# Feed-forward products of a decoder step by one level of Strassen's algorithm, up units first

## The chip, the cores and the metric

The kernel runs on one core of a Trainium2 chip. The time is that of the whole launch on the device in microseconds (us), as a median over runs; lower is better. Engines are named as the profile names them: PE is TensorE, with PEld for its weight loads, DVE is VectorE, ACT is ScalarE, POOL is GpSimd, and SP is SyncE, which here only issues transfers.

## The reference

One step of a gated decoder layer for 1024 prompt tokens and 8 x 8 sample tokens, all in float32, 1088 token columns in all:

```
u = rmsnorm(x);  [a | q | k | v | g_a | g_b] = u @ w_in            # w_in: 1024 x 4864
A = causal multi-scale pooling of a  @ w_pa
B = dilated sliding-window attention of q, k, v and the caches  @ w_pb
h = x + (sigmoid(g_a) * A + sigmoid(g_b) * B) @ w_o                # 1024 x 1024
y = h + relu(rmsnorm(h) @ w_up)^2 @ w_down                         # 1024 x 4096, 4096 x 1024
```

Outputs are y and the updated pooling states and key-value caches. The last two lines are what the change touches.

## The kernel before

All of it works on transposed activations: 128 channels on the partitions, tokens along the free axis. The 1088 tokens are cut into CHUNKS of 384, 384 and 320 columns. Every matmul operand is held as two fp32r parts, a high and a low one, and every product is made in three passes (high by high, high by low, low by high; `PASSES`, L132, `gemm`, L141 to L150, the matmul in L148). `split` (L104 to L107) makes the parts: ACT copies the value into the high part (L105), DVE subtracts that from the value for the low part (L106).

Weights come in panels of 128 x 2048 (`panel`, L114 to L127): four transfers of 256 KB on SP's queue, each split into one of three rotating `places`. `throttle` collects the last split of each panel; the copies of the caches to the outputs (L1202 to L1212, 44 transfers of some 1 MB on POOL's queue) wait for one such split each, from the fourteenth on, so that they go out one to a panel.

The stage of w_o (L1132 to L1152) makes `y` = h in SBUF, one tile of 128 x 1088 for each of eight channel blocks, chunk by chunk, and sums its squares into `sqa`. In its last panel and in the first feed-forward unit the closures in `todo` are called between the matmuls, one chunk at a time: `norm_sums` (column sums of `sqa` by PE, mean on DVE, power -1/2 on POOL), `split_h` (h times ln2, split into `act[0]` and `act[1]`), and `norm_spread` (a diagonal matrix on DVE, spread over the partitions by PE, copied to `rbh` by ACT).

The feed-forward loop (L1156 to L1199) has 16 units f, each for 256 of the 4096 hidden channels. An up half: the panel of w_up, six `gemm`s `pz` (three chunks by two blocks, 24 matmuls each), then r = max(pz, 0) * rbh on DVE (L1180), the square's high part on ACT (L1181), and its low part by two DVE operations (L1182, L1183) into `z`. A down half follows at once: the panel of w_down, 24 `gemm`s `py` of six matmuls each, and each sum is added to `y` in place by DVE (L1199). The last unit adds into rows in token order and stores them as `yT` (L1192 to L1196). Each half is 144 matmuls.

PE's instructions stand in the order of the code. On the other engines, the order is set when the program is built, by a scheduler that models times; each engine then takes its queue strictly in order, and transfers of one queue are issued in order, each waiting for what its buffers need.

Of the kernel before, what the change touches and what calls it, by code (L numbers as in the profile page):

```python
# [7 lines left out]
F32 = mybir.dt.float32  # L8
F32R = mybir.dt.float32r
# [23 lines left out]
def decoder_step(ctx, tc, i, o):  # L33
# [17 lines left out]
    cst = cp.tile([P, i["consts"].shape[1]], F32, name="cst")  # L51
    cols = cp.tile([P, i["cols"].shape[1]], F32, name="cols")
    off = [0]

    def take(n):
        r = cst[:, off[0]:off[0] + n]
        off[0] += n
        return r

    ident, m1, m3, halves, hmask, icnt, ms0, ms1, hsel, bsel = (take(n) for n in (128, 256, 128, 64, 1, 15, 136, 136, 4, 4))  # L60
# [39 lines left out]
    places = wp.tile([P, 3, 2, 2048], F32R, name="places")  # L100
    place = [0]
# [60 lines left out]
    acc_p = pool("acc", space=PSUM)  # L162
# [30 lines left out]
    xp = pa.enter_context(tc.tile_pool(name="pooling", bufs=1, side="right", reuse_waits="tile"))  # L193
    ap0 = pb.enter_context(tc.tile_pool(name="att0", bufs=1, reuse_waits="tile"))
# [165 lines left out]
    dma(cst, i["consts"])  # L360
# [731 lines left out]
    yp = pool("y", reuse_waits="tile")  # L1092
    y = [yp.tile([P, TOK], F32, name=f"y{k}") for k in range(KD)]
    rbh = yp.tile([P, TOK], F32, name="rbh")
    pd = ExitStack()
    hp = pd.enter_context(tc.tile_pool(name="h", bufs=1, side="right", reuse_waits="tile"))
    ps = pd.enter_context(tc.tile_pool(name="ps_d", bufs=1, space=PSUM, reuse_waits="tile"))
    sqa = [hp.tile([P, n], F32, name=f"sqa{c}") for c, (c0, n) in enumerate(CHUNKS)]
    hms = hp.tile([P, 9], F32, name="hms")
    hr = hp.tile([P, 9], F32, name="hr")  # L1100
    v_.memset(hr, 0.0)

    def norm_sums(c):
        n = CHUNKS[c][1]
        rt = ps.tile([P, 3], F32, name=f"rth{c}", tag="rt")
        for b in range(3):
            w = min(P, n - b * P)
            t_.matmul(rt[:w, b:b + 1], sqa[c][:, b * P:b * P + w], ones[:, :1], start=True, stop=True)
        for b, w in ((slice(0, n // P), P), (slice(n // P, 3), n % P)):
            if w and b.stop > b.start:  # L1110
                col = slice(3 * c + b.start, 3 * c + b.stop)
                v_.tensor_scalar(hms[:w, col], rt[:w, b], 1.0 / D, EPS, op0=ALU.mult, op1=ALU.add)
                g_.tensor_tensor(hr[:w, col], hms[:w, col], mhalf[:w, b], op=ALU.pow)

    def norm_spread(c):

        c0, n = CHUNKS[c]
        dg = rr(hp, [P, 3, P], F32, name=f"dg{c}", tag="dg", bufs=1)
        bc = ps.tile([P, 512], F32, name=f"bc{c}", tag="bc")
        spread(dg, hr, c, bc)  # L1120
        s_.copy(rbh[:, c0:c0 + n], bc[:, :n])

    def split_h(c):
        c0, n = CHUNKS[c]
        for k in range(KD):
            hi, lo = (act[s][k][:, c0:c0 + n] for s in range(2))
            behind_pe(s_.activation(hi, y[k][:, c0:c0 + n], AF.Copy, scale=ln2[:, k:k + 1]))
            v_.scalar_tensor_tensor(lo, y[k][:, c0:c0 + n], ln2[:, k:k + 1], hi.bitcast(F32),
                                    op0=ALU.mult, op1=ALU.subtract)

    todo = []
    for d in range(4):  # L1132
        wt = by_k(panel(i["w_o"][d], f"o{d}"))
        xr = rr(hp, [P, 2, TOK], F32, name=f"xr{d}", tag="xr", bufs=2)
        dma(xr, i["xT"][:, 2 * d:2 * d + 2])
        for c, (c0, n) in enumerate(CHUNKS):
            for m in range(2):
                kk = 2 * d + m
                po = acc_tile(f"ph{kk}_{c}")
                gemm(po[:, :n], KD, lambda s, k: wt[:, s, k, m * P:(m + 1) * P], lambda s, k: act[s][k][:, c0:c0 + n])  # L1140
                for here, row, toks in pieces(c):
                    v_.tensor_tensor(y[kk][:, row], po[:, here], xr[:, m, toks], op=ALU.add)
# [13 lines left out]
    NG = 16  # L1156
    fp = None
    for f in range(NG):
        wt = by_k(panel(i["w_up"][f], f"u{f}"))
        zz = []  # L1160
        for c, (c0, n) in enumerate(CHUNKS):
            pzs = []
            for m in range(2):
                pz = acc_tile(f"pz{f}_{c}_{m}")
                gemm(pz[:, :n], KD, lambda s, k: wt[:, s, k, m * P:(m + 1) * P], lambda s, k: act[s][k][:, c0:c0 + n])
                pzs.append(pz)
                if todo:
                    todo.pop(0)()
            if fp is None:
                while todo:  # L1170
                    todo.pop(0)()
                pd.close()
                fp = ctx.enter_context(tc.tile_pool(name="ffn", bufs=1, side="right", reuse_waits="tile"))
                ps = ctx.enter_context(tc.tile_pool(name="ps_e", bufs=1, space=PSUM, reuse_waits="tile"))
            z = rr(fp, [P, 2, 2, CH], F32R, name=f"z{f}_{c}", tag="z", bufs=4)
            zz.append(z)
            for m in range(2):
                r = rr(fp, [P, CH], F32, name=f"r{f}_{c}_{m}", tag="r", bufs=2)
                q = rr(fp, [P, CH], F32, name=f"q{f}_{c}_{m}", tag="q", bufs=2)
                v_.scalar_tensor_tensor(r[:, :n], pzs[m][:, :n], 0.0, rbh[:, c0:c0 + n], op0=ALU.max, op1=ALU.mult)  # L1180
                s_.activation(z[:, m, 0, :n], r[:, :n], AF.Square)  # L1181
                v_.tensor_tensor(q[:, :n], r[:, :n], r[:, :n], op=ALU.mult)  # L1182
                v_.tensor_tensor(z[:, m, 1, :n], q[:, :n], z[:, m, 0, :n].bitcast(F32), op=ALU.subtract)  # L1183
        wt = by_k(panel(i["w_down"][f], f"d{f}"), 2)
        final = f == NG - 1
        for c, k in [(c, k) for k in range(KD) for c in range(3)] if final else [(c, k) for c in range(3) for k in range(KD)]:
# [3 lines left out]
            if final:  # L1190

                row = y[k - 1] if k else rbh  # L1192
                for here, cols_, toks in pieces(c):
                    v_.tensor_tensor(row[:, toks], y[k][:, cols_], py[:, here], op=ALU.add)
                if c == 2:
                    dma_st(o["yT"][k * P:(k + 1) * P], row)  # L1196
# [115 lines left out]
```

## Time and profile before

| what | value |
|---|---|
| median of 3 runs | 1545.11 us (1544.89 to 1545.24) |
| span of the profiled execution, first to last instruction | 1543.0 us |
| time outside that span, against the median | 2.1 us |
| feed-forward stage, 32 halves of one unit | 757.9 us of the span |
| bytes moved by DMA | 178.66 MB, 116 GB/s on average |

The page gives busy times by engine over the span, the chain of work that ended last, groups of instructions with their mean durations, and the idle time ahead of them with what ended it. Busy times are averages over stages of very different kinds: attention keeps DVE, ACT and POOL busy, the feed-forward stage hardly uses POOL. What the change is worth is read from the feed-forward stage and its two ends.

### The profile page before, as it was taken

How to read it: one execution, taken by the hardware profiler on the slowest of the kernel's cores; microseconds unless marked ns; L12 is line 12 of the kernel's file. 1: busy time of each engine (PE TensorE's matmuls, PEld its weight loads, DVE VectorE, ACT ScalarE, POOL GpSimd, SP SyncE). 2: the span in 40 equal slices, each digit the busy share in tenths (PEclk: the TensorE clock that was granted, in tenths of full speed). 3: DMA queues.
4: the chain of work that ended last, by engine and by line, in shares of the span. 5: the costliest groups of instructions: out<-in, count | busy, mean ns of one | idle time of the engine just before them, and what ended most of it. 6: DMA issues, size and time to landing. Idle time of an engine off the chain costs nothing.

```text
span 1543.0 us, 25508 instructions
## 1 busy us (share of the span) xinstructions
PE 1519.3 (98%) x9779; PEld 1475.6 (96%) x9779; DVE 875.1 (57%) x1948; ACT 516.2 (33%) x1613; POOL 199.4 (13%) x245
## 2 busy tenths in 40 slices
PE   8999799899999999999999999999999999999998
PEld 8989788778999999999999999999999999999998
DVE  7555555858755444344575565555655556555556
ACT  8466655667763222222241111211111211112100
POOL 2611256545200000010010000000000000000000
PEclk9999899999999999999999999999999999999999
DMA  6212667765445443574331322313213223222102
GB/s 216 87 48 75 175 159 180 214 173 124 124 125 174 157 147 120 182 230 156 109 100 60 107 80 79 106 54 106 99 60 106 75 89 109 68 95 99 35 8 117
DMA packets 104536, 178.66 MB, mean 116 GB/s; under 512 B 16919, under 2 KB 69725, under 8 KB 103198
## 3 DMA queue, kind: packets, MB, share of 16 engines
q1 hardware_dynamic: 97870, 125.91, 27.0%
q0 software_dynamic: 6112, 50.33, 9.8%
q8 instruction: 77, 1.26, 0.3%
q10 hardware_dynamic: 432, 0.79, 0.1%
q14 instruction: 45, 0.37, 0.1%
HBM read 155.54 MB, written 65.10 MB: 143 GB/s over the span
## 4 chain that ended last, share of the span: by engine, by line
PE 92%; DMA 3%; DVE 2%; ACT 1%; issue 1%; POOL 1%; SPq 0%; DVEq 0%; POOLq 0%; ACTq 0%
PE py L148 25%; PE pz L148 24%; PE pga L148 6%; PE pgb L148 6%; PE ph L148 6%; PE pqk L148 5%; PE pv L148 3%; PE a L260 3%; PE pa L148 3%; DMA raw_qkv<-in_w_in_dram 2%; PE pb L148 2%; PE pk L148 1%; PE pq L148 1%; PE pog0b L623 1%; DMA pck<-in_cache_kv_dram 1%
## 5 line engine op out<-in xcount | busy, mean ns | idle before, releaser
L148 PE MATMUL pz<-act,places 128*128 128x384 f32 (+1 forms) x2304 | 382.4, 326 | 0.0
L148 PE MATMUL py<-z,places 128*128 128x384 f32 (+1 forms) x2304 | 381.6, 327 | 0.0
L148 PEld LDWEIGHTS pz<-act,places 128*128 128x128 f32 x2304 | 379.5, 188 | 0.4
L148 PEld LDWEIGHTS py<-z,places 128*128 128x128 f32 x2304 | 379.7, 188 | 0.0
L1199 DVE TENSOR_TENSOR y<-y,py 128x384 f32<-128x384 f32 (+1 forms) x360 | 187.9, 530 | 111.5 <-PE py L148 111.2
L1181 ACT ACTIVATE z<-r 128x384 fp32r<-128x384 f32 (+1 forms) x96 | 48.7, 508 | 321.9 <-DVE r L1180 321.9
L1180 DVE SCALAR_TENSOR_TENSOR r<-pz,rbh 128x384 f32<-128x384 f32 (+1 forms) x96 | 51.2, 534 | 168.8 <-PE pz L148 168.8
L1210 POOL DMA_DIRECT2D out_kv_sample_dram<-in_cache_kv_dram x44 | 21.8, 494 | 932.4 <-ACT places L105 910.8
L105 ACT ACTIVATE places<-raw_u 128x512 fp32r<-128x512 f32 x64 | 38.4, 627 | 266.9 <-PE py L148 258.6
L148 PE MATMUL pga<-act,places 128*128 128x384 f32 (+1 forms) x576 | 97.9, 328 | 0.0
L148 PE MATMUL pgb<-act,places 128*128 128x384 f32 (+1 forms) x576 | 97.8, 326 | 0.0
L148 PE MATMUL ph<-act,places 128*128 128x384 f32 (+1 forms) x576 | 95.9, 327 | 0.0
L148 PEld LDWEIGHTS pgb<-act,places 128*128 128x128 f32 x576 | 95.4, 188 | 0.0
L148 PEld LDWEIGHTS ph<-act,places 128*128 128x128 f32 x576 | 94.8, 188 | 0.3
L148 PEld LDWEIGHTS pga<-act,places 128*128 128x128 f32 x576 | 94.6, 188 | 0.3
L556 POOL TENSOR_TENSOR mr<-ms,mhalf 128x4 f32<-128x4 f32 (+2 forms) x39 | 49.8, 1277 | 113.0 <-DVE ms L555 107.5
L148 PE MATMUL pqk<-places,act 128*128 128x512 f32 x240 | 60.7, 402 | 0.0
L1183 DVE TENSOR_TENSOR z<-q,z 128x384 fp32r<-128x384 f32 (+1 forms) x96 | 51.3, 535 | 10.6 <-DVE q L1182 3.2
L106 DVE TENSOR_TENSOR places<-raw_d,places 128x512 fp32r<-128x512 f32 x64 | 41.4, 689 | 24.1 <-ACT places L105 24.1
L260 PE MATMUL a<-act,places 128*128 128x384 f32 (+1 forms) x288 | 51.2, 338 | 2.9 <-ACT act L242 2.8
L148 PEld LDWEIGHTS pqk<-places,act 128*128 128x128 f32 x240 | 44.5, 191 | 9.7 <-issue 0.2
L260 PEld LDWEIGHTS a<-act,places 128*128 128x128 f32 x288 | 49.5, 193 | 3.8 <-ACT act L242 3.4
(296 smaller groups left out, 2030.1 us busy)
## 6 DMA issues: line engine op xcount, KB each, us to landing
out_kv_sample_dram<-in_cache_kv_dram POOLq DMA_DIRECT2D x36, 960.0 KB, 5.6
raw_u<-in_w_up_dram SPq DMA_DIRECT2D x64, 256.0 KB
raw_d<-in_w_down_dram SPq DMA_DIRECT2D x64, 256.0 KB
raw_qkv<-in_w_in_dram SPq DMA_DIRECT2D x36, 256.0 KB
pck<-in_cache_kv_dram SPq DMA_DIRECT2D x32, 256.0 KB
pcv<-in_cache_kv_dram SPq DMA_DIRECT2D x32, 256.0 KB
out_kv_sample_dram<-in_cache_kv_dram POOLq DMA_DIRECT2D x8, 1008.0 KB, 5.5
kts<-in_kT_dram SPq DMA_DIRECT2D x20, 256.0 KB
```

The lines of the kernel that those rows point to most:

```text
L105: ins = s_.activation(dst_hi, src, AF.Copy)
L106: v_.tensor_tensor(dst_lo, src, dst_hi.bitcast(F32), op=ALU.subtract)
L148: last_mm[0] = t_.matmul(out, lhs(a, k), rhs(b, k), start=(j == 0), stop=(j == len(terms) - 1))
L260: last_mm[0] = t_.matmul(pts[m][:, :n], wt[:, a, kk, m * P:(m + 1) * P], act4[b][kk][:, :, part4(c)], start=(p == 0 and kk == 0), stop=(p ...
L556: g_.tensor_tensor(r[:n, :H], ms[:n, :H], mhalf[:n, :H], op=ALU.pow)
L623: t_.matmul(po[:, h * HD:(h + 1) * HD], pTs[e][:, hp * nk + j, :], vr[:, h * HD:(h + 1) * HD], start=(j == 0), stop=(j == nk - 1))
L1180: v_.scalar_tensor_tensor(r[:, :n], pzs[m][:, :n], 0.0, rbh[:, c0:c0 + n], op0=ALU.max, op1=ALU.mult)
L1181: s_.activation(z[:, m, 0, :n], r[:, :n], AF.Square)
L1183: v_.tensor_tensor(z[:, m, 1, :n], q[:, :n], z[:, m, 0, :n].bitcast(F32), op=ALU.subtract)
L1199: v_.tensor_tensor(yc, yc, py[:, :n], op=ALU.add)
L1210: ins = g_.dma_start(d, a)
```

## The change

One level of Strassen's algorithm (the form with 15 additions) is used for both feed-forward products. A unit of w_up is split into four quarters (two halves of its 1024 input channels, two blocks of 128 output channels), the tokens into two halves of 544. Seven products M1 to M7, each of one weight quarter or sum of quarters by one activation quarter or sum, replace eight. Each product is made for two runs of 272 columns, with 12 matmuls each (four channel blocks by three passes), in a pair of PSUM banks; PSUM also does some of the sums, since several products of one unit accumulate in the same banks.

- All 16 up units come first. The fourth product's work of a unit (M4) is `owed`: it stands after the second product of the next unit.
- Weight sums (`made` in `prep_up`, four of 128 x 512 a unit) and four sums of the squared results (`sub` in `up_done`) are POOL's. The seven quarters or sums `z` of each unit are split and stored to `z_d` in DRAM (`keep`, seven transfers of 128 x 1088), on SP's queue.
- The activations' sums T1 to T4 (`diff`, on POOL and DVE) and all their splits stand between w_o's last panel and unit 0. That panel is done in four row blocks of 272 columns instead of three chunks. The norm's sums are taken once for all columns, after M1 of unit 0, and spread after its M2.
- h goes to `h_d` in DRAM and is added back later (`add_h`, eight times), on POOL.
- The down units work on two hidden blocks (iterations t-1 and t, half of each iteration's blocks of y at a time): 12 matmuls per product, 84 per unit, with half units of 42 at t = 0 and t = 16. They load z from DRAM (`load_z`) into the tiles that the activations and weights held before, and w_down in one transfer of 1 MB (`load_down`).
- The cache copies that wait for the fourteenth to the twenty-seventh panel now go two to a panel.
- The constants are loaded in two transfers, so that most of them are freed after attention.

```diff
-    for d in range(4):
...
-            if d == 3:
-                todo += [lambda c=c: (norm_sums(c), split_h(c)), lambda c=c: norm_spread(c)]
...
-    for f in range(NG):
-        wt = by_k(panel(i["w_up"][f], f"u{f}"))
...
+        for c0, n in CHUNKS if d < 3 else [(r * R4, R4) for r in range(4)]:
...
+                squares(kk, slice(c0, c0 + n), n)
...
+            if d == 3 and c0 == R4:
+                for k in range(4):
+                    split(act[0][k][:, h0], act[1][k][:, h0], y[k][:, h0])
...
+    def product(pt, n_k, w, z, start):
+        for s in range(2):
+            terms = [(a, b, k) for a, b in PASSES for k in range(n_k)]
+            for j, (a, b, k) in enumerate(terms):
+                last_mm[0] = t_.matmul(pt[:, s, :R4], w(a, k), z(b, k, s), start=(start and j == 0),
+                                       stop=(j == len(terms) - 1), skip_group_check=True)
...
+    def order_of(f):
+        return ("M1", "M5", "M6", "M2", "M3", "M7") if f else ("M1", "M2", "M5", "M6", "M3", "M7")
...
+        def made(m, a, b, op=ALU.subtract):
+            src[m] = temp(f"s{m}_{f}").rearrange("p (k c) -> p k c", k=4)
+            g_.tensor_tensor(src[m], a, b, op=op)
...
+    def keep(f, m, src):
+        st = gp.tile([P, 2, H], F32R, name=f"zs{f}_{m}", tag=f"g{stage[0] % 4}", bufs=1)
+        stage[0] += 1
+        src = src.rearrange("p s l -> p (s l)")
+        split(st[:, 0], st[:, 1], src)
+        dma_st(z_d[f][AT[m]], st.rearrange("p b l -> p (b l)").bitcast(F32))
...
+        def done(m, p1, p2, p3):
+            if m == "M1":
+                q["11"] = quarter("q11", 1, f"q11_{f}")
+                s_.copy(q["11"], p1)
...
+            if m == "M2":
+                v_.tensor_tensor(q["11"], p3, q["11"], op=ALU.add)
+                squared(q["11"], q["11"], 0)
+                keep(f, "M1", q["11"])
...
+                sub(q["t1"], q["12"], q["11"])
...
+            def first_done(m, *p):
+                if m == "M1":
+                    norm_sums()
+                    p1_first.append(p)
+                elif m == "M2":
+                    spread_and_open()
...
+    for t in range(NG + 1):
+        if t:
+            load_z(t + 1)
+            load_down(t + 1)
+        ts = [0] if t == 0 else [t - 1] if t == NG else [t - 1, t]
...
+        for j in (0, 2) if t % 2 else (1, 3):
+            w = prep_down(j, ts)
+            unit(f"d{t}_{j}", len(ts), lambda m, a, q, w=w: w[:, IN_SET[m], a, q], down_z(ts),
+                 down_done(j, t >= NG - 1), order_of(NG))
+            if dd is None:
...
+                load_z(1)
+                load_down(1)
...
-    late = throttle[13:]
+    late = [p for p in throttle[13:27] for _ in range(2)] + throttle[27:]
```

Two places where the order changes. The first is SP's queue at the change from up to down units. Before, at the last units, it holds only weight pieces (`raw_u`, `raw_d`), each for the half that comes next:

```order
L111 DMA raw_u15_0_14997<-in_w_up_dram 128x512
L111 DMA raw_u15_512_15001<-in_w_up_dram 128x512
L111 DMA raw_u15_1024_15005<-in_w_up_dram 128x512
L111 DMA raw_u15_1536_15009<-in_w_up_dram 128x512
L111 DMA raw_d15_512_15206<-in_w_down_dram 128x512
L111 DMA raw_d15_0_15202<-in_w_down_dram 128x512
L111 DMA raw_d15_1024_15210<-in_w_down_dram 128x512
L111 DMA raw_d15_1536_15214<-in_w_down_dram 128x512
```

Now SP's queue has, at the end of a row of loads for z0 to z2 (`act` and `places` from `z_d`), a piece of h (`hback0`), the last unit's stores (`zs15`), four pieces of z2 and z3 that go into new tiles (`zc`), and behind them the w_down block of iteration 1 (`rd1`):

```order
L1504 DMA hback0_14051<-h_d_7907 128x1088
L1310 DMA z_d15_4_8017<-zs15_M3_12922 128x1088
L1310 DMA z_d15_2_8015<-zs15_M6_12928 128x1088
L1310 DMA z_d15_5_8018<-zs15_M7_12933 128x1088
L1310 DMA z_d15_3_8016<-zs15_M2_12999 128x1088
L1310 DMA z_d15_6_8019<-zs15_M4_13004 128x1088
L1425 DMA zc2_6_13123<-z_d2_6_7928 128x1088
L1425 DMA zc3_0_13349<-z_d3_0_7929 128x1088
L1425 DMA zc3_1_13351<-z_d3_1_7930 128x1088
L1425 DMA zc3_2_13353<-z_d3_2_7931 128x1088
L1438 DMA rd1_13052<-in_w_down_dram 128x2048
```

What moved: the load of the down weights stands behind 37 stores and loads, counted from the first load of z, where a panel's load stood right behind that of the panel before.

The second place is DVE between w_o's last panel and unit 0. Before, for chunk 0 while chunk 1 of the panel is multiplied (`ph6_1`, `ph7_1` are chunk 1's products, `rth0` chunk 0's column sums, `dg0` its diagonal matrix, `act1` the low parts of h):

```order
L1148 TENSOR_TENSOR sqa0_7919<-sqa0_7919,hq7_0_8588 128x384
L1142 TENSOR_TENSOR y6_7910<-ph6_1_8591,xr3_8529 128x160
L1142 TENSOR_TENSOR y6_7910<-ph6_1_8591,xr3_8529 128x224
L1112 TENSOR_SCALAR hms_7922<-rth0_8621 128x3
L1128 SCALAR_TENSOR_TENSOR act1_73<-y0_7904,cols_59,act0_72 128x384
L1128 SCALAR_TENSOR_TENSOR act1_73<-y1_7905,cols_59,act0_72 128x384
L185 TENSOR_TENSOR dg0_8673<-cst_58,hr_7923 128x384
L1128 SCALAR_TENSOR_TENSOR act1_73<-y2_7906,cols_59,act0_72 128x384
L1128 SCALAR_TENSOR_TENSOR act1_73<-y3_7907,cols_59,act0_72 128x384
L1128 SCALAR_TENSOR_TENSOR act1_73<-y4_7908,cols_59,act0_72 128x384
L1128 SCALAR_TENSOR_TENSOR act1_73<-y5_7909,cols_59,act0_72 128x384
L1128 SCALAR_TENSOR_TENSOR act1_73<-y6_7910,cols_59,act0_72 128x384
```

Now DVE has there, after the last product of w_o (`ph7_816`), the splits of T1 and T2 (`act1`, `t2`), the last squares' sum (`hq7_816`), four more splits, and the means (`hms` from `norms`, PE's column sums):

```order
L94 TENSOR_TENSOR act1_64<-y1_8026,act0_63 128x544
L94 TENSOR_TENSOR act1_64<-y2_8027,act0_63 128x544
L94 TENSOR_TENSOR act1_64<-y3_8028,act0_63 128x544
L1138 TENSOR_TENSOR t2_2_8041<-y6_8034,y2_8027 128x544
L94 TENSOR_TENSOR act1_64<-t2_0_8039,act0_63 128x544
L94 TENSOR_TENSOR act1_64<-t2_1_8040,act0_63 128x544
L1130 TENSOR_TENSOR sqa_8043<-sqa_8043,hq7_816_8924 128x272
L94 TENSOR_TENSOR t4_0_8996<-y4_8032,t4_0_8996 128x544
L94 TENSOR_TENSOR t4_1_9000<-y5_8033,t4_1_9000 128x544
L94 TENSOR_TENSOR places_68<-y6_8034,places_68 128x544
L94 TENSOR_TENSOR places_68<-ru1_9012,places_68 128x512
L1290 TENSOR_SCALAR hms_8044<-norms_9011 128x8
```

What moved: the means stood behind one chunk's two additions and ahead of its splits; now they stand behind the last square, which stands behind the six splits and the subtraction, and behind four more splits.

More of the change, by code (lines that the diff above doesn't have):

```diff
@@ L50, in decoder_step @@
     cp = pool("const")
-    cst = cp.tile([P, i["consts"].shape[1]], F32, name="cst")
+    ident = cp.tile([P, P], F32, name="ident")
     cols = cp.tile([P, i["cols"].shape[1]], F32, name="cols")
[L53 to L60, printed above, removed]
     ln1, ln2, pscale, wqc = cols[:, 0:8], cols[:, 8:16], cols[:, 16:20], cols[:, 20:26]
@@ L100, in decoder_step @@
     places = wp.tile([P, 3, 2, 2048], F32R, name="places")
+    room = places.rearrange("p n s c -> p (n s c)")
     place = [0]
@@ L1101, in decoder_step @@
     v_.memset(hr, 0.0)
[L1103 to L1129, printed above, removed]
@@ L1156, in decoder_step @@
-    NG = 16
-    fp = None
-    for f in range(NG):
-        wt = by_k(panel(i["w_up"][f], f"u{f}"))
[L1160 to L1186, printed above, removed]
-            c0, n = CHUNKS[c]
-            py = rr(ps, [P, CH], F32, name=f"py{f}_{c}_{k}", tag="py", bufs=4)
-            gemm(py[:, :n], 2, lambda s, m: wt[:, s, m, k * P:(k + 1) * P], lambda s, m: zz[c][:, m, s, :n])
[L1190 to L1196, printed above, removed]
-            else:
-                yc = y[k][:, c0:c0 + n]
-                v_.tensor_tensor(yc, yc, py[:, :n], op=ALU.add)
@@ new lines, in decoder_step, with norm_sums @@
+    for k in range(4):
+        diff(g_, k, "t3")
+        split(t3[k // 2][:, k % 2, 0], t3[k // 2][:, k % 2, 1], y[k][:, h0])
+    for k in range(4):
+        diff(g_, k, "t4")
+        t4.append(cell(f"c{k}", [P, 2, H], F32R, f"t4_{k}"))
+        split(t4[k][:, 0], t4[k][:, 1], y[4 + k][:, h0])
+    norms = pair(turns["spare"], "norms")
+    def norm_sums():
+        rt = norms[:, 1, 384:393]
+        for b in range(9):
+            w = min(P, TOK - b * P)
+            t_.matmul(rt[:w, b:b + 1], sqa[:, b * P:b * P + w], ones[:, :1], start=True, stop=True)
+        for b, w in ((slice(0, 8), P), (slice(8, 9), TOK % P)):
+            v_.tensor_scalar(hms[:w, b], rt[:w, b], 1.0 / D, EPS, op0=ALU.mult, op1=ALU.add)
+            g_.tensor_tensor(hr[:w, b], hms[:w, b], mhalf[:w, :b.stop - b.start], op=ALU.pow)
@@ L1202, in decoder_step @@
+    owed.pop()()
+    ctx.enter_context(pz_)
     shifts = []
```

350 lines of the change are left out of this document (324 added, 26 removed).

## The prediction

> **What bounds the kernel now.** I read the page's busy times first, then the chain that ended last, then the feed-forward part alone.
>
> ```profile
> span 1543.0 us, 25508 instructions
> PE 1519.3 (98%) x9779; PEld 1475.6 (96%) x9779; DVE 875.1 (57%) x1948; ACT 516.2 (33%) x1613; POOL 199.4 (13%) x245
> PE 92%; DMA 3%; DVE 2%; ACT 1%; issue 1%; POOL 1%; SPq 0%; DVEq 0%; POOLq 0%; ACTq 0%
> ...
> 760.00:1500.00 740.00, 739.62 (x4498) 738.61 (x4498) 422.78 (x801) 132.46 (x244) 17.80 (x32) 1.00 0.24 80
> ...
> 1490.70 23.68 PE pz L148 x144
> 1514.37 23.88 PE py L148 x144
> ```
>
> TensorE carries 92% of the chain. In the window row (its columns: stretch, length, busy time and count of PE, weight loads, DVE, ACT and POOL, granted clock, DMA share, GB/s) it idles for 0.4 of 740 us, and DVE is busy for 57%. The last two rows are one up and one down unit in the chain: 144 matmuls in 23.68 us, back to back; the chain lists 32 such pieces, 757.9 us together. So a matmul saved there is time saved, as long as everything that feeds TensorE keeps its cover. The median of 1545.1 is 2.1 us above the span; I forecast the span and add 2.1.
>
> **Removed and added matmuls.** Strassen takes 7 half products for 8, but in tiles of 272 columns where 384 and 320 stood: 16 up units of 168 matmuls, 30 down units of 84 (each takes the halves of two iterations together) and four of 42 at the two ends; together 5376 matmuls for 4608. What one of 272 columns costs has no row; three sizes near it have, as runs of 24 weight loads from the first start to the next group's:
>
> ```profile
> 650.72 4.17 PEld L148 LDWEIGHTS pgb<-act,places 128*128 128x128 f32 x24
> 654.88 0.36 PEld L148 LDWEIGHTS pa<-ab,places 128*128 128x128 f32 x2
> ...
> 665.28 3.58 PEld L148 LDWEIGHTS pgb<-act,places 128*128 128x128 f32 x24
> 668.82 0.51 PEld L148 LDWEIGHTS pa<-ab,places 128*128 128x128 f32 x3
> ...
> 259.65 2.89 PEld L148 LDWEIGHTS pq<-places,act 128*128 128x128 f32 x24
> 262.48 0.53 PEld L623 LDWEIGHTS pog1b<-v,pTg1b 128*128 128x128 f32 x4
> ```
>
> 384 columns: 4.16/24 = 173.3 ns. 320: 3.54/24 = 147.5. 256: 2.83/24 = 117.9. Down from 320 by the slope of the upper two (0.403 ns a column) 272 costs 128.2; up from 256 by the same slope 124.4; I take 127.3, nearer the 320 row, whose slope I trust; bounds 118 and 147.5. 5376 x 0.1273 = 684.4, so **-73.5**. The last w_o panel is done in four row blocks of 272 for three chunks: 192 x 0.1273 = 24.4 for 23.7, **+0.7**.
>
> **Work beside TensorE.** Per up unit, a cover of 168 x 0.1273 = 21.4 us:
>
> ```profile
> L1199 DVE TENSOR_TENSOR y<-y,py 128x384 f32<-128x384 f32 x240 | 130.8, 552 | 79.8 <-PE py L148 79.5
> L1199 DVE TENSOR_TENSOR y<-y,py 128x320 f32<-128x320 f32 x120 | 57.2, 486 | 31.7 <-PE py L148 31.7
> L106 DVE TENSOR_TENSOR places<-raw_u,places 128x512 fp32r<-128x512 f32 x60 | 39.9, 687 | 4.4 <-ACT places L105 3.5
> L1142 DVE TENSOR_TENSOR y<-ph,xr 128x272 f32<-128x272 f32 x3 | 1.9, 638 | 2.1 <-PE ph L148 2.1
> L105 ACT ACTIVATE places<-raw_u 128x512 fp32r<-128x512 f32 x60 | 36.1, 627 | 266.2 <-PE py L148 258.6 <-DMA raw_u<-in_w_up_dram 7.6
> ...
> 342.41 2.33 POOL L763 TENSOR_TENSOR pcv<-pcv,sc 128x256 f32<-128x256 f32 x4 [1.07 <-DMA pcv<-in_cache_kv_dram]
> ...
> 31.99 2.38 DVE L106 TENSOR_TENSOR places<-raw_a,places 128x512 fp32r<-128x512 f32 x1 [2.41 <-ACT places L105]
> 36.77 9.82 POOL L234 TENSOR_TENSOR xs<-xs,xs 128x768 f32<-128x768 f32 x5 [0.69 <-ACT xs L232]
> 41.21 5.92 DVE L106 TENSOR_TENSOR places<-raw_qkv,places 128x512 fp32r<-128x512 f32 x3 [3.98 <-ACT places L105]
> ```
>
> DVE: 7 weight remainders of 512 at 0.69, and 14 of 544 at 0.72 (0.552 plus 160 columns at the 1.03 ns between the first two rows): 14.9 us. ACT has 21 operations at about 0.65, 13.7. Both fit. POOL, nearly idle here before (17.8 us in 740), gets 4 sums of 512 and 4 of 544: at 0.58 for 256 columns (2.33/4), in proportion, 1.17 and 1.24, together 9.6. But the last three rows show POOL and DVE in each other's way: a DVE subtraction of 512 from two SBUF operands takes 0.69 alone and 5.92/3 = 1.97 beside POOL's long subtractions. The trace shows this for two SBUF operands, and 17 of DVE's 21 operations have those (12.1 us; the others read PSUM); if these and POOL's 9.6 take turns, 21.7 a unit; if all of DVE's do, 24.6. In the 5.38 us that both ran from 41.21, POOL's 2.7 operations (5.38/1.96; alone 1.75 by the columns) and DVE's 3 make 6.9 us of work in the 5.9 that DVE took, so they overlap a little rather than lose time: I take 21.7, 0.3 over the cover, 16 units: **+5** (0 to +51).
>
> DMA in an up unit: seven stores of 128x1088 (0.557 MB) and 1.05 MB of weights, 4.9 MB in 21.4 us, 231 GB/s. POOL's cache copies (0.96 MB each, read and written) now come two to a panel where one stood, until the up units, which issue one each; the panel of w_o in the third row below would go from 265 GB/s by 1.92 MB in 23.7 us to 346, below the best rate of the trace, so 0 (to +3):
>
> ```profile
> 10.00:20.00 10.00, 10.00 (x51) 10.00 (x51) 10.00 (x14) 10.00 (x16) 0.00 (x0) 0.86 1.07 373
> 170.00:190.00 20.00, 12.13 (x68) 10.07 (x68) 9.05 (x34) 11.58 (x56) 5.81 (x8) 0.66 0.74 188
> ...
> 684.00:707.70 23.70, 23.70 (x146) 23.70 (x145) 11.74 (x25) 6.91 (x13) 0.50 (x1) 1.00 0.71 265
> ...
> q1 hardware_dynamic: 97870, 125.91, 27.0%
> ```
>
> 373 GB/s with all DMA engines busy in the first; by the last, 125.91 MB in 27% of 1543 us, 302 GB/s of mean rate. Stores and loads are covered in the steady state of both stages. A down unit (10.7 us on TensorE) asks DVE for 7 x 0.72 + 4 x 0.69 = 7.8 and POOL for eight pieces of 128 columns, 2.3: covered. The two half units of the last iteration have 42 matmuls, 5.3 us, and on DVE 7 x 0.72 + 4 x 0.36 = 6.5: **+2** for both. The end after the last matmul (one sum, one store) stays as it is.
>
> **Seam one, w_o to unit 0.** Before, sums, power and spread of the norm came chunk by chunk between w_o's matmuls. Now one norm for all columns stands behind M1 of unit 0. From the end of the second w_o row block TensorE has 96 + 24 matmuls, 15.3 us, until the sums; DVE in its order has 19 subtractions of 544 (13.7), 5 additions of `y` (0.64 each, 3.2) and 5 of squares (0.44 each, 2.2) up to the last square that the sums wait for: 19.1, so 4 us of idle, up to 18 if POOL's 11 subtractions of 1.24 in that stretch delay it in full. Then in series: four splits queued ahead of the means on DVE (2.8), the power on POOL, further splits, and three spreads whose scale matrices are interleaved with four more:
>
> ```profile
> L556 POOL TENSOR_TENSOR mr<-ms,mhalf 128x8 f32<-128x8 f32 x15 | 25.3, 1688 | 51.0 <-DVE ms L555 50.7
> L1113 POOL TENSOR_TENSOR hr<-hms,mhalf 64x1 f32<-64x1 f32 x1 | 0.8, 808 | 0.0
> L185 DVE TENSOR_TENSOR dg<-cst,hr 128x384 f32<-128x384 f32 x3 | 1.7, 558 | 0.5 <-POOL hr L1113 0.5
> ```
>
> 2.8 + 0.2 + 1.7 + 0.8 + 1.0 (the rest of five splits that run beside the power) + 3 x 0.56 + 4 x 0.72 + 0.5 for TensorE = 11.6, of which M2 covers 3.1: 8.5. Together 12.5 to 27; **+19**, the middle, since rows show both delayed and undisturbed subtractions.
>
> **Seam two, unit 15 to the down units.** Iteration 1 of the down units needs its w_down block `rd1`. On SP's queue it stands behind 37 transfers that may start when M5 of unit 15 frees the first slots (48 matmuls, 6.1 us into the unit): loads of z0 to z2, part of z3, the last stores and a piece of h. 36 x 0.557 + 1.05 = 21.1 MB at 373 GB/s take 56.6 us, so it lands at 62.7; POOL's sums (2.3) and the split (1.3) make 66. TensorE has until then 168 + 60 + 42 matmuls, 34.4 us: **+32**. From below: were the loads all ahead of time, the queue would still wait for the last stores, M4's (its product ends at 204 x 0.1273 = 26, then about 7 for its two rounds of DVE, ACT, POOL and a store), four loads and `rd1` (8.7) and 3.6: stall 11. From above, at 302 GB/s: 45. I take 32, because the queue is issued in order. Some 50 us of TensorE idle in both seams also lets the granted clock fall: 0.66 where it was busy for 12 of 20 us (second row above), so **+3** (0 to 6).
>
> **Sum.** -73.5 + 0.7 + 5 + 2 + 19 + 32 + 3 = -11.8; 1543.0 - 11.8 + 2.1 = 1533.3.
>
> **Rivals.**
> *The seams are mostly hidden* (0.2): seam two costs 11 and seam one 12, clock 1: -73.5 + 0.7 + 5 + 2 + 24 = -41.8, **1503**. For it: 16 DMA engines take several transfers at once; against: one queue, and 21 MB are 21 MB.
> *POOL and DVE become the bound of the up units* (0.18; the other side): if all of DVE's work and POOL's take turns, 24.6 us a unit for 21.4, +51 where I have +5: **1579**. It decides from 22.3 us a unit on (8.9 us more than my sum). For it: 1.97 for 0.69 above; against: the 6.9 us of work in 5.9. The Trainium skill, "SBUF — State Buffer", section "Who interferes with whom", says that a DVE instruction with two SBUF inputs contends with a GpSimd instruction that reads SBUF, while one with a single SBUF input doesn't; by that rule it is the 21.7 and not the 24.6, and the trace's stretched subtraction agrees with its first half.
> *Slower transfers* (0.09): 302 GB/s in seam two, +13: **1546**.
> *272 columns cost as much as 320* (0.03): 5376 x 0.0202 more, +109: 1642.
>
> **How the numbers follow.** My forecast, 1533, has 0.5, and its own range is 1518 to 1548 (seam one from 12 to 27, seam two 11 to 45, with little chance that both ends meet). No change means within 0.2%, 1542 to 1548.2, about what a measurement of this kernel can tell. Faster: 0.7 of my case, the hidden seams: 0.35 + 0.2 = 0.55. Same: 0.1, from my case's upper end and the slower transfers. Slower: the rest, 0.35. For 8 in 10 the range reaches into both large rivals, 1502 to 1570; a full 24.6 a unit and the 320-column price stay out.
>
> **What would show it.** Right: up units 21.4 to 22 us apart and gapless; an idle TensorE of some 19 us in two pieces around M2 of unit 0; one of some 30 us before the first unit of iteration 1, released by POOL or ACT behind the landing of `rd1`, with DMA saturated above 350 GB/s before it; down units 10.7 us apart. Wrong: TensorE waits in every up unit for a split or a subtraction, with DVE's 512 subtraction well over 0.69 and POOL's 544 over 1.24 (second rival); a 272 run of 24 off 3.06 us; or `rd1` landing early.

## The result: 1.3% slower, and the profile after

The changed kernel took 1564.05 us (median of 4, 1562.56 to 1570.29) beside 1545.17 us for the kernel before (4 runs): ratio 1.0129, interval 1.011 to 1.0147. Forecast were 1533 and a range up to 1570; the time lies in the range, but it went the other way than forecast.

The first lines of the page after, with the span, the engines' busy times and the chain by engine:

```profile
span 1562.0 us, 28183 instructions
PE 1458.1 (93%) x10595; PEld 1403.0 (90%) x10595; DVE 1021.3 (65%) x1812; ACT 685.8 (44%) x1885; POOL 577.9 (37%) x649
...
PE 58%; DMA 12%; DVE 10%; POOL 9%; ACT 5%; issue 4%; SPq 0%; POOLq 0%; ACTq 0%; DVEq 0%
```

TensorE is busy for 61 us less than before, while the span is 19 us longer. It carried 92% of the chain; now 58%, and POOL, nearly idle in this part before, carries 9%. What TensorE waited for (the view of waits; columns: us in total, number of waits, the longest):

```profile
PE p1d L1198 <- ACT places L93: 29.0, 1, 29.0
PE p1u L1198 <- ACT q L1327: 16.5, 13, 2.9
PE p1u L1198 <- ACT q L1330: 11.5, 12, 1.0
PE norms L176 <- DVE dg L174: 7.1, 3, 5.6
...
PE norms L1288 <- DVE sqa L1130: 3.3, 1, 3.3
PE p1u L1198 <- DVE y L1160: 2.9, 1, 2.9
```

The first row is the change from up to down units, one wait. The next two are the up units: nearly every unit waits once before M6 for ACT's copy of M1 (L1327) and once before M7 for that of M6 (L1330). The next two are the norm between w_o and unit 0, and in the last M1 of unit 0 waits for DVE's additions behind w_o. The matmuls themselves got cheaper than forecast, here 24 in an undisturbed down unit (weight loads):

```profile
1236.29 3.06 PEld L1198 LDWEIGHTS p1d<-act,places 128*128 128x128 f32 x24
1239.29 0.81 PEld L1198 LDWEIGHTS p3d<-act,places 128*128 128x128 f32 x6
```

3.00/24 = 125 ns; over the whole stage 125.4. So the account of the 19 us in the two profiled executions, from the starts of TensorE's products, is:

| part | forecast | measured |
|---|---|---|
| 5376 matmuls of 272 for 32 pieces of 23.68 | -73.5 | -83.8 (674.1 for 757.9) |
| w_o to unit 1, beyond unit 0's matmuls | +19, and part of +3 | +26.9, less 2.3 that the same stretch cost before beyond its 32 pieces (the norm's matmuls among it): +24.6 |
| up units, beyond their matmuls | +5 | +36.4 (352.4 for 316.0; 15 units of 23.5) |
| change to down units, waits | +32, and part of +3 | +33.9 |
| down units and the rest | +2 and +0.7 | +8 |
| sum | -11.8 | +19 |

One term stands out: the up units.

Their groups on DVE and POOL between 860 and 1150 us (columns: count, busy time, mean ns of one, idle time before):

```profile
L94 DVE TENSOR_TENSOR zs_M<-q,zs_M 128x544 fp32r<-128x544 f32 x61 | 67.6, 1108 | 29.6 <-ACT zs_M L93 27.9
L94 DVE TENSOR_TENSOR places<-sM,places 128x512 fp32r<-128x512 f32 x49 | 56.6, 1155 | 7.3 <-ACT places L93 7.3
...
L1315 DVE SCALAR_TENSOR_TENSOR q<-p1u,rbh 128x544 f32<-128x544 f32 x12 | 8.5, 711 | 0.0
...
L1322 POOL TENSOR_TENSOR t<-q,t 128x544 f32<-128x544 f32 x12 | 22.1, 1844 | 0.0
```

DVE's subtractions of two SBUF operands take 1.11 and 1.16 us on average for 0.72 and 0.69, its operation with one operand in PSUM 0.711 as computed, and this one of POOL's subtractions 1.84. And ACT's queue around one wait before M6 (timeline: start, length, and in brackets the idle time before and what ended it):

```profile
1016.80 0.63 ACT L93 ACTIVATE places<-ru 128x512 fp32r<-128x512 f32 x1 [0.72 <-DMA ru<-in_w_up_dram]
1017.34 0.64 ACT L93 ACTIVATE zs_M<-q 128x544 fp32r<-128x544 f32 x1
...
1017.88 0.59 ACT L1327 COPY q<-p1u 128x544 f32<-128x544 f32 x1
...
1018.53 0.65 PE L1198 MATMUL p1u<-act,places 128*128 128x272 f32 x3 [1.57 <-ACT q L1327]
```

The copy of M1 stands behind the first split of the next unit's weights, which waits for them to land; TensorE waits for the copy. Of the eight units between 900 and 1100 us, three have this wait of TensorE too, of 0.7 us each, though the split there waits for nothing.

Ahead of M7 it is alike, with DVE and POOL at its head:

```profile
999.97 1.59 DVE L94 TENSOR_TENSOR zs_M<-q,zs_M 128x544 fp32r<-128x544 f32 x1
...
1000.94 1.77 POOL L1242 TENSOR_TENSOR sM<-ru 128x512 f32<-128x512 f32 x1
...
1001.48 0.71 DVE L1315 SCALAR_TENSOR_TENSOR q<-p1u,rbh 128x544 f32<-128x544 f32 x1
...
1002.23 0.66 ACT L1316 ACTIVATE q<-q 128x544 f32<-128x544 f32 x1 [1.78 <-DVE q L1315]
...
1004.01 0.59 ACT L1330 COPY q<-p1u 128x544 f32<-128x544 f32 x1
```

A subtraction of DVE is stretched beside POOL's (1.59 us). The next operation on DVE, with an operand in PSUM, is not (0.71 us, wholly beside POOL's), but it comes late. ACT's square waits 1.78 us for it, and the copy of M6 (L1330) stands behind this square and two splits.

### The profile page after: what moved, and what is told of

It is laid out like the page before. It is cut to its first block, busy times and chain, and to the rows that moved or that the text cites. A ratio compares the mean times of both kernels' runs of the same rounds, so it can differ in the third digit from the quotient of the medians.

```text
span 1562.0 us, 28183 instructions
## 1 busy us (share of the span) xinstructions
PE 1458.1 (93%) x10595; PEld 1403.0 (90%) x10595; DVE 1021.3 (65%) x1812; ACT 685.8 (44%) x1885; POOL 577.9 (37%) x649
## 4 chain that ended last, share of the span: by engine, by line
PE 58%; DMA 12%; DVE 10%; POOL 9%; ACT 5%; issue 4%; SPq 0%; POOLq 0%; ACTq 0%; DVEq 0%
PE p1d L1198 11%; PE pgb L136 6%; PE pga L136 6%; PE p2d L1198 5%; PE pqk L136 5%; DMA ru<-in_w_up_dram 5%; PE ph L136 4%; PE a L264 3%; POOL q L1322 3%; PE pa L136 3%; PE pv L136 3%; PE p3d L1198 3%; POOL sM L1242 2%; DVE zs_M L94 2%; ACT zs_M L93 2%
## 5 line engine op out<-in xcount | busy, mean ns | idle before, releaser
L1198 PE MATMUL p1d<-act,places 128*128 128x272 f32 x1104 | 195.4, 290 | 32.2 <-ACT places L93 29.0
L1198 PEld LDWEIGHTS p1d<-act,places 128*128 128x128 f32 x1104 | 165.6, 190 | 33.7 <-ACT places L93 29.2
L1198 PE MATMUL p1u<-act,places 128*128 128x272 f32 x768 | 105.9, 295 | 19.4 <-ACT q L1327 16.5
L1198 PEld LDWEIGHTS p1u<-act,places 128*128 128x128 f32 x768 | 101.1, 194 | 22.4 <-ACT q L1327 19.3
L1548 POOL DMA_DIRECT2D out_kv_sample_dram<-in_cache_kv_dram x44 | 22.3, 509 | 264.0 <-ACT places L93 251.4
L94 DVE TENSOR_TENSOR zs_M<-q,zs_M 128x544 fp32r<-128x544 f32 x80 | 84.6, 1057 | 50.8 <-ACT zs_M L93 48.9
L1198 PE MATMUL p1u<-t,places 128*128 128x272 f32 x768 | 103.0, 290 | 11.8 <-ACT q L1330 11.5
L1198 PEld LDWEIGHTS p1u<-t,places 128*128 128x128 f32 x768 | 98.3, 188 | 14.7 <-ACT q L1330 14.1
L1499 DVE TENSOR_TENSOR yd<-yd,p1d 128x544 f32<-128x544 f32 x116 | 83.0, 716 | 39.2 <-PE p1d L1198 39.2
L1198 PE MATMUL p2d<-act,places 128*128 128x272 f32 x528 | 97.5, 289 | 4.2 <-ACT q L1316 1.7
L136 PE MATMUL ph<-act,places 128*128 128x384 f32 (+2 forms) x624 | 95.4, 314 | 0.0
```

Of the source, the lines that this page charges most:

```text
L94: v_.tensor_tensor(dst_lo, src, dst_hi.bitcast(F32), op=ALU.subtract)
L136: last_mm[0] = t_.matmul(out, lhs(a, k), rhs(b, k), start=(j == 0), stop=(j == len(terms) - 1))
L1198: last_mm[0] = t_.matmul(pt[:, s, :R4], w(a, k), z(b, k, s), start=(start and j == 0), stop=(j == len(terms) - 1), skip_group_check=True)
L1499: v_.tensor_tensor(part, part, p[src], op=ALU.add)
L1548: ins = g_.dma_start(d, a)
```

## The experiments

All kernels below are the changed kernel with edits. Each median is given beside the runs of the kernel before on the same chip (1543.4 to 1544.8 us).

**1. The w_down block ahead of z2 and z3 on the queue.** In `load_z` (and alike for the tile that is loaded in two pieces):

```diff
-                dma(dst.bitcast(F32), z_d[t][n])
+                ld = dma(dst.bitcast(F32), z_d[t][n])
+                if t in (2, 3):
+                    tc.add_manual_dep(ld.ins, rd_ins[1].ins.name, mybir.DependencyInfo(
+                        mybir.DependencyClass.Sync, mybir.DependencyReason.DATA), reason="pace")
```

> The changed kernel, with one thing moved: the loads of z2 and z3 wait until the w_down block of iteration 1 (rd1) has landed, so that on SP's queue rd1 stands directly behind the last stores of the up units instead of behind eleven more loads. Theory (order on the queue): the 29 us wait of TensorE between the first and second down iteration is transfer time of what stands ahead of rd1; 11 of 37 transfers (6 MB of 21, 16 us at 373 GB/s) go behind it, so the wait falls to 8 to 14 us and the time to about 1545 (1540 to 1550). Rival (the last stores end it): rd1 may start only when the last z of unit 15 is stored, and those stores are late for another reason than bytes; then the wait stays above 24 us and the time within 5 us of 1564.

1553.37 us (ratio 1.0055, 1.0035 to 1.0076). The one wait before the first unit of iteration 1:

```profile
PE p1d L1198 <- ACT places L93: 14.7, 1, 14.7
```

Half of the 29 us was the place on the queue, so that part is shown; the rest was not, and the time gained, 11 us, is less than forecast. The chain of this kernel there shows what is left:

```profile
1175.16 11.34 DMA z_d<-zs_M
...
1186.56 10.65 DMA z_d<-zs_M
...
1198.67 5.08 DMA z_d<-zs_M
...
1203.80 6.14 DMA rd<-in_w_down_dram
```

```profile
1178.00:1185.00 7.00, 4.99 (x28) 4.58 (x27) 6.36 (x10) 3.90 (x7) 1.35 (x1) 0.80 1.01 403
1185.00:1190.00 5.00, 5.00 (x40) 5.00 (x39) 4.23 (x6) 3.56 (x7) 3.96 (x3) 0.94 1.03 421
```

A store of 0.557 MB takes 11 us in this stretch, while DMA moves 403 and 421 GB/s (last column of the second fence, windows of the same kernel), and the last results wait for a stage tile, then for the last store, before `rd1` may begin.

**2. `rd1` by ACT, into free space.** Besides edit 1, `rd1` is issued by ACT and lands where the up units' quarters were, so that it needs no tile of the stores (`zc` and the rows of the result change sides for it):

```diff
-        dma(r, i["w_down"][t].rearrange("p (m c) -> p m c", m=2))
+        rd_ins[t] = (s_.dma_start if t == 1 else dma)(r, i["w_down"][t].rearrange("p (m c) -> p m c", m=2))
...
-                dd = pr.enter_context(tc.tile_pool(name="wdown", bufs=1, reuse_waits="tile"))
+                dd = pr.enter_context(tc.tile_pool(name="wdown", bufs=1, side="right", reuse_waits="tile"))
```

> As the kernel in which z2 and z3 wait for rd1, and besides rd1 is issued by ACT, not SP, into space that the up units' results leave free, not the stores' tiles. So it waits no more for the last store of unit 15 to land. Theory (15 us were left there because rd1 waits for that last store, 5 us after its split, and its own 6 us): the wait falls from 15 to about 9 us, time about 1547 beside 1553. Rival (DMA at 400 to 420 GB/s until then: z0, z1, 11 stores and rd1 are 15 MB, 37 us from M5 of unit 15 at that rate): the landing hardly moves, the wait stays above 13 us.

1548.69 us (1.0034, 1.0021 to 1.0046); the wait was 13.8 us for 14.7. The rival's number came true, but this run doesn't show that bytes set the rest. The chain:

```profile
1181.42 10.64 DMA z_d<-zs_M
...
1195.00 0.01 ACT zs_M L93
1195.01 7.32 DMA rd<-in_w_down_dram
```

On ACT's queue `rd1` stands behind the last split of unit 15, and that waits, by way of one more split, DVE and POOL, for a store of 10.6 us to free its stage tile. So `rd1` still set off behind the stores, 5.8 us into TensorE's wait where it had been 7.8, and then took 7.3 us for 6.1. No run separates its place on ACT's queue from the bytes.

**3. The norm one product later.** The sums after M2, the spread after M5:

```diff
                 if m == "M1":
+                    p1_first.append(p)
+                elif m == "M2":
                     norm_sums()
                     p1_first.append(p)
-                elif m == "M2":
+                elif m == "M5":
                     spread_and_open()
                     done("M1", *p1_first[0])
+                    done("M2", *p1_first[1])
                     done(m, *p)
```

> The changed kernel, with the norm of unit 0 one product later: column sums after M2 instead of M1, spread after M5 instead of M2. Theory (TensorE waits in series for the norm): each of the two waits (3.4 us for the last square, 5.9 us for the first diagonal matrix) gets 3.0 us more cover, so 6 us less, 1558. Rival (backlog: DVE and ACT have a fixed amount of splitting to do in unit 0, and TensorE waits for that wherever the norm stands): the copies of M1, M2 and M5 and the products M6 and M3 wait instead, and the time stays within 2 us of 1564.

1567.36 us (1.0148, 1.0122 to 1.0174). My theory (1558) fell; the time lies 3 us above the changed kernel's, and the rival's 2 us are missed as well. The waits in the norm:

```profile
PE norms L176 <- DVE dg L174: 11.4, 3, 9.8
...
PE norms L1288 <- DVE sqa L1130: 1.2, 1, 1.2
```

The wait for the last square fell from 3.3 to 1.2 us, and that for the diagonal matrix rose from 5.6 to 9.8: as in the rival, TensorE waits for the work that DVE, ACT and POOL have in front of them, though here in the norm itself.

**4. T3 and T4 on DVE.** Two edits: `diff(g_, k, "t3")` and `diff(g_, k, "t4")` become `diff(v_, ...)`. The reason was one DVE operation of the changed kernel:

```profile
795.45 2.92 POOL L1291 TENSOR_TENSOR hr<-hms,mhalf 128x8 f32<-128x8 f32 x2
...
797.87 4.72 DVE L174 TENSOR_TENSOR dg<-ident,hr 128x384 f32<-128x384 f32 x1
798.35 1.32 POOL L1138 TENSOR_TENSOR y<-t,y 128x544 f32<-128x544 f32 x1
799.63 1.33 POOL L1138 TENSOR_TENSOR y<-y,t 128x544 f32<-128x544 f32 x1
...
800.92 1.26 POOL L1242 TENSOR_TENSOR sM<-ru 128x512 f32<-128x512 f32 x1
```

The matrix, 0.55 us elsewhere, stretches over three POOL operations that follow each other without a gap, and ends 0.4 us after the last of them.

> The changed kernel, with the eight subtractions for T3 and T4 between w_o and unit 0 on DVE instead of POOL (undisturbed 0.72 us each). Theory (DVE's operations with two SBUF operands wait for POOL's: the first diagonal matrix took 4.72 us for 0.56 while POOL worked without a gap): the matrix falls below 1 us, the wait before the spread from 5.9 to 2 us, and the splits before it get shorter; seam one falls by 3 to 7 us, 1559. Rival (DVE's backlog is what TensorE waits for): 8 x 0.72 = 5.8 us more of it, up to 1570.

1563.14 us (1.013, 1.0114 to 1.0146). The longest wait before the spread fell from 5.6 to 3.8 us, and the one for the last square rose from 3.3 to 5.6; the stretch from w_o to unit 1 was 25.2 us for 26.9, no more than kernels differ that don't touch it (24.6 to 29.2). The matrix's stretch is real; it fell to 2.15 us, not below 1, and that bought nothing here: DVE has the subtractions instead.

**5. The results' sums on DVE.** In `sub` of `up_done`:

```diff
-            g_.tensor_tensor(out, a, b, op=ALU.subtract)
+            v_.tensor_tensor(out, a, b, op=ALU.subtract)
```

> The changed kernel, with the four sums of the squared results in each up unit on DVE instead of POOL (the four sums of weights stay on POOL). DVE then has 25 operations of 0.69 to 0.72 a unit, 17.8 us of 21.1 if undisturbed. Theory (shared access of DVE and POOL to SBUF: DVE's splits take 1.0 to 1.17 us for 0.7 beside POOL): splits fall below 0.9 us, the 32 us that TensorE waits in the up units fall to 10, time about 1543. Rival 1 (ACT's queue order: the copy of M1 stands behind a split that waits for the next weights): the waits before M6 (18.6 us of the 32) stay, time 1555 to 1560. Rival 2 (DVE becomes the bound): slower than 1564.

1559.19 us (1.0091, 1.0074 to 1.0108). The waits before M7 are gone, those before M6 grew from 16.5 to 24.7:

```profile
PE p1u L1198 <- ACT q L1327: 24.7, 11, 5.7
```

The 15 units from the second on took 350.0 us; in the kernels that don't touch them (the changed one and those of 1 to 4) they took 349.9 to 354.4, so nothing was gained there. DVE's splits did get shorter, those of the weights that came from POOL to 0.69 us. That is rival 1: ACT's queue order keeps the unit at 23.3 us.

**6. The first split after M6.** In `prep_up`, from unit 2 on, the split for M1 waits until M6 of the unit before has ended:

```diff
             ins = split(w[:, 0], w[:, 1], src[m])
+            if f > 1 and m == "M1":
+                behind_pe(ins, m6_last[f - 1])
```

> The changed kernel, with one thing moved: from unit 2 on the first weight split of an up unit waits until M6 of the unit before has ended, so that ACT's copy of M1 (which M6 waits for) no longer stands behind a split that waits for the weights to land. Theory (ACT's queue order): the 13 waits before M6, 18.6 us together, fall to about 3; the waits before M7 (13.4 us) stay; time about 1549. Rival (throughput of DVE and POOL sets the pace of a unit, 23.7 us): the same microseconds come back as waits at M7, M1 or M4, and the time stays within 4 us of 1564.

1559.76 us (1.0094, 1.0073 to 1.0114). The waits before M6 (L1332 in this kernel) fell to 3.9 us as the theory has it, those before M7 (L1335) rose from 11.5 to 14.3:

```profile
PE p1u L1198 <- ACT q L1335: 14.3, 13, 2.2
...
PE p1u L1198 <- ACT q L1332: 3.9, 11, 0.4
```

The 15 units took 342.6 us, 22.8 a unit: 10 us less than in the changed kernel, of which the time shows 4.3, since the stretches ahead of and behind them came out 4 us longer in this profile. Neither the theory's 1549 nor the rival's full return came. Alone, neither edit is worth more than 5 us by the medians.

**7. Both.** Edits 5 and 6 together.

> The two edits to the up units together: the four sums of results on DVE, and the first weight split of a unit behind M6 of the unit before. Apart, the first took away the waits before M7 (13 us to 0) and raised those before M6 to 27, the second took the waits before M6 from 19 to 6 and raised those before M7 to 16. Theory (two causes: POOL and DVE in each other's way ahead of M7, ACT's queue order ahead of M6): the savings add, TensorE waits under 8 us in the up units, 1564 falls to about 1539 (1535 to 1545), the first version below or beside the kernel before. Rival (one common limit, the throughput of DVE and POOL): the waits move again, 20 us or more are left in the up units, and the time stays above 1550.

1526.06 us (0.989, 0.9872 to 0.9908): 38 us below the changed kernel by the medians (37 by the ratios), where 5 and 4 apart. The rival (one common limit) fell, and the theory's saving was too small. The window from 860 to 1130 us of the changed kernel and of this one (columns as in the first window row):

```profile
860.00:1130.00 270.00, 245.11 (x1899) 240.51 (x1898) 217.78 (x238) 136.72 (x235) 150.40 (x100) 0.99 0.69 248
```

```profile
860.00:1130.00 270.00, 270.00 (x2155) 270.00 (x2154) 242.98 (x318) 153.67 (x266) 83.59 (x71) 1.00 0.81 283
```

2155 matmuls for 1899, and TensorE never waits: a unit takes its 21.1 us. Beside experiment 5 only the place of that split on ACT and DVE differs, beside experiment 6 only the place of the results' sums, and each is worth 33 us here. A unit was held up by whichever of two limits came later, so taking away one showed the other.

**8. The cache copies out of the up units.** `throttle[27:]` becomes `throttle[44:]`.

> The changed kernel, with the 16 cache copies that go out one an up unit (0.96 MB, read and written) moved to the down units. Theory (the load of w_up is slow because it shares the DMA engines: 7 to 9.5 us in the chain for 1 MB, 2.8 at 373 GB/s): the load falls to about 5.5 us, the waits before M6 fall by 10 to 15 us, time about 1552. Rival (the load's time is its turn behind the stores of z on the same queue): the load stays above 7 us, and the time within 4 us of 1564.

1567.02 us (1.0158, 1.014 to 1.0177). The load of w_up, 22% of the chain from 860 to 1150 us of the changed kernel, is no longer in the chain: thirteen such loads landed 4.6 to 5.9 us after their issue, where they took 6.3 to 9.6. The rival's load above 7 us fell, but the waits before M6 are as long, so the theory's time fell too:

```profile
PE p1u L1198 <- ACT q L1327: 17.3, 13, 1.8
```

What holds the copy of M1 now shows in four rows:

```profile
1012.31 1.74 POOL L1242 TENSOR_TENSOR sM<-ru 128x512 f32<-128x512 f32 x1
...
1012.82 1.81 DVE L1315 SCALAR_TENSOR_TENSOR q<-q,rbh 128x544 f32<-128x544 f32 x1
...
1014.66 0.66 ACT L1316 ACTIVATE q<-q 128x544 f32<-128x544 f32 x1 [1.62 <-DVE q L1315]
...
1016.29 0.59 ACT L1327 COPY q<-p1u 128x544 f32<-128x544 f32 x1
```

With the weights there earlier, POOL's first sum meets a DVE operation of two SBUF operands that had taken 0.71 us undisturbed; it takes 1.81, and ACT's square, ahead of the copy, waits 1.62 us for it where it had waited 0.5. So what the chain named at its head was not what set the pace: with the load faster, the unit waits as long for DVE and POOL.

**9. Idle work on POOL.** To see POOL's hindrance apart from waits for its results, the kernel of 7 got work that nobody reads:

```diff
             g_.tensor_tensor(src[m], a, b, op=op)
+            for n in (0, 2) if f > 1 else ():
+                g_.tensor_tensor(room[:, 12000:12256].rearrange("p (k c) -> p k c", k=2), src[m][:, n:n + 2],
+                                 rbh[:, :256].rearrange("p (k c) -> p k c", k=2), op=ALU.subtract)
```

> The kernel with both edits to the up units, and from unit 2 on, behind each of the four sums of weights on POOL, two more subtractions of 128x256 with two SBUF operands, whose result nobody reads: 8 a unit, 0.58 us each if undisturbed, 4.6 us a unit, about what the four sums of results cost POOL before they went to DVE. The order of instructions on DVE, ACT and SP is the same as without them, so nothing waits for them except POOL's own later sums. Theory (POOL's work as such takes DVE's access to SBUF): DVE's 25 operations a unit get slower by about as much, 17.8 + 4 x 1.5 + 4.6 = 28 of 21.1 us, TensorE waits again by 3 to 7 us a unit, and 1526 becomes 1565 to 1620. Rival (what hurt was that results came late through POOL's queue): within 4 us of 1526.

1576.52 us (1.0224, 1.0203 to 1.0245), 50 us more than without. Rows of DVE and POOL:

```profile
L94 DVE TENSOR_TENSOR zs_M<-q,zs_M 128x544 fp32r<-128x544 f32 x59 | 69.4, 1177 | 7.2 <-ACT zs_M L93 6.5
...
L1321 DVE SCALAR_TENSOR_TENSOR q<-p1u,rbh 128x544 f32<-128x544 f32 x12 | 8.5, 711 | 0.0
...
L1245 POOL TENSOR_TENSOR places<-sM,rbh 128x256 fp32r<-128x256 f32 x94 | 102.9, 1095 | 3.9
```

DVE's subtractions are back at 1.18 us (0.91 without the idle work), its operation with a PSUM operand, which runs beside POOL's in all twelve units, stays at 0.711, and a unit takes 24.4 us. (The profiled execution was the slowest of the four, 1583.41 us.)

**10. The same with fills.** `g_.memset` of 128x256, four behind each sum of weights, 16 a unit.

> As the kernel with idle subtractions on POOL, but the idle work only writes: behind each of POOL's four sums of weights four fills of 128x256 with zero, 16 a unit, again with the same order of instructions on DVE, ACT and SP. The Trainium skill, SBUF — State Buffer, section Who interferes with whom, says that a DVE instruction with two SBUF inputs contends with a GpSimd instruction that reads SBUF, not with one that only writes it. Theory (the reads are what hinders DVE; POOL's delay of its own sums costs nothing): DVE's durations stay as without idle work (0.82 to 1.05 us for its splits), and the time within 4 us of 1526. Rival (any work on POOL does it, by delaying POOL's own sums or by holding DVE up): over 1540, if the fills keep POOL busy for 4 us a unit or more.

1543.64 us (0.9996, 0.9983 to 1.0009), 18 us more than without by the medians (16 by the ratios). Three operations of DVE, the first beside a POOL subtraction, the others beside fills:

```profile
1009.83 1.53 POOL L1243 TENSOR_TENSOR sM<-ru,sM 128x512 f32<-128x512 f32 x1
1010.13 1.77 DVE L94 TENSOR_TENSOR places<-sM,places 128x512 fp32r<-128x512 f32 x1
1011.29 2.53 POOL L1245 MEMSET places<- 128x256 f32 x7
...
1011.83 0.71 DVE L1322 SCALAR_TENSOR_TENSOR q<-p1u,rbh 128x544 f32<-128x544 f32 x1
...
1012.46 0.68 DVE L94 TENSOR_TENSOR places<-ru,places 128x512 fp32r<-128x512 f32 x1
```

Beside fills DVE's subtraction of two SBUF operands takes 0.68 us, beside a subtraction 1.77. Over the window from 860 to 1150 us, 51 such operations of DVE ran beside fills for at least half their time, and beside none of POOL's sums; they took 0.67 to 0.73 us each. This half of the theory is shown, and agrees with the Trainium skill, "SBUF — State Buffer", section "Who interferes with whom", which lets only a GpSimd instruction that reads SBUF contend with a DVE instruction of two SBUF inputs. The other half fell: fills cost 18 us without holding DVE up. What is left is that they delay POOL's own sums of weights; that is inferred, no row shows it alone. So of the 50 us of experiment 9 some part is that delay too, and how much isn't settled.

**11. All.** Edits 1, 2, 5 and 6.

> Both edits to the up units, and both to the down weights (z2 and z3 behind rd1; rd1 issued by ACT into free space). The up units wait for nothing, and the wait at the change to down units falls from 30 to about 14. Theory (the two stretches are independent): 1526 - 16 = 1510 (1506 to 1515). Rival (with faster up units the stores and loads around the change have less time, and DMA at 400 GB/s is the bound there): the wait stays above 22 us, 1518 or more.

1510.88 us (0.9793, 0.9771 to 0.9815): the two stretches are independent, the wait at the change to down units was 14.7 us, and this version is 2.1% faster than the kernel before (1.9 to 2.3).

## Why the prediction was wrong, step by step

- **Matmuls (-73.5): right, too small.** 272 columns cost 125.4 ns, between the 124.4 and 128.2 that the rows bracketed; measured -83.8.
- **Work beside TensorE (+5): this step failed;** it measured +36.4. It compared sums with the cover: 21.7 us a unit of operations of DVE and POOL that take turns, and ACT's 13.7, against 21.4. That DVE and POOL hinder each other stood in it. What failed is the sum as the measure of a wait, and a wait that it put at nothing, ACT's.
- **The sum itself was a little small, but that isn't the cause.** I had scaled POOL's costs by columns from short operations, 1.17 and 1.24 us. POOL's rows in experiment 4, undisturbed while DVE's matrix waits, are 1.26 and 1.32 to 1.33: 4 x 1.26 + 4 x 1.33 = 10.4 for 9.6, so 22.5, over the cover of 21.1, since the matmuls were faster as well. That would be +21 over 15 units, and 22.5 lies near the 22.8 of experiment 6. The traces don't bear it out as the limit. Worked out from the starts and lengths of the operations in units 4 to 14, at least one operation of POOL or one of DVE with two SBUF operands is running for 20.3 us a unit in the changed kernel, where a unit takes 23.8, and for 20.4 of 23.2 in experiment 6. Both are under the cover: the turns overlap a little, as the prediction read from its rows, and neither engine was used up. So the nearness of 22.5 to 22.8 is luck.
- **What the runs showed in its place: the order of ACT's queue, fed by late results (23.5 us a unit for 21.1).** The copies of M1 and M6 stand in one queue with squares and splits that wait for DVE, POOL and transfers, and TensorE waits for the copies: 28 us of idle time in the two rows of waits, and 31.5 of the 36.4 us at these places when counted from start to start of its matmuls. DVE's and POOL's operations stretch each other (1.1 to 1.8 us for 0.7, 1.8 for 1.33), so that what ACT waits for comes late; experiment 8 shows one such wait replaced by another. Experiments 5 to 7 show that the results' sums had to leave POOL and the split had to move before the waits were gone. How much of POOL's part is stretched operations and how much is results that come late through its queue stays open (experiments 9 and 10). In experiment 9 DVE itself is nearly full, busy for 255 of the 270 us from 860 to 1130.
- **Rival 2 (0.18) came nearest.** It said 1579 by 24.6 us a unit and named 22.3 as the point where it decides; the unit took 23.5. Its mechanism was half right: operations of DVE with a PSUM operand were not hindered (0.71 us beside POOL), turns of both engines didn't fill the unit, and ACT's order was no part of it. That its number lies near is luck too.
- **Seam two (+32): right**, 33.9, for the reason given: 37 transfers ahead of `rd1`. Experiment 1 shows half of it as queue order. The rest is a store that the last results wait for and `rd1`'s own 6 to 7 us, both slow among many transfers, with ACT's queue in experiment 2; I had treated all of it as one sum of bytes.
- **Seam one (+19): a little small**, 24.6 with the slower clock. After waits TensorE took 4.78 and 5.80 us from the first start to the last end of M1 and M2 of unit 0, whose 24 matmuls take 3.2 later. The granted clock was 0.64 in the first and 0.50 in the second, and 0.71 in the whole stretch; with M5 (4.67 us) that is some 5.7 us, where +3 stood for both seams:

```profile
779.80:821.70 41.90, 30.80 (x168) 27.51 (x169) 31.22 (x43) 20.28 (x38) 13.74 (x7) 0.71 0.14 52
```

- **Down units (+2):** 8; 30 units with short waits that I hadn't counted.

The range held the time, since it reached to the second rival; that it held is luck, since the mechanism of that rival is not what the runs showed. The sign went wrong by one term of the sum, 31 us too small.

## What to carry to other kernels

Moving work to an idle engine is not free when it shares operand access with a busy one: here the operations of both got longer and their results came later. Adding up their times and comparing with the cover didn't tell it, since the engines were not full and TensorE waited all the same. Before calling an engine's queue covered, look at what stands ahead of the one instruction that TensorE waits for, and at what each of those waits for. And when two edits each give little, run them together before dropping either: here 5 and 4 us apart made 38.

## What the runs showed of the hardware that I had not expected

- A DVE operation with two SBUF operands can be held up over several POOL operations in a row: 4.72 us for 0.55 until POOL paused. POOL pays as well: its 544-column subtraction took 1.8 us beside DVE's for 1.33, and one, at 788.44 us of the changed kernel, 5.26 us while DVE's operations followed each other.
- POOL's fills, in contrast, leave such an operation at 0.68 us, and a DVE operation with one operand in PSUM stays at 0.71 beside POOL's subtractions.
- 403 and 421 GB/s, in two windows of 7 and 5 us, were moved at the change to down units, above the 373 that I had as the best rate.
